# The order of two pieces of work in an FFN block: the next block's first hidden chunk and the second product's first weight block

## The chip, the cores and the metric

The kernel runs on one core of a Trainium2 chip. The metric is device time in microseconds (us) from the first to the last instruction, with what the launch adds around it; several executions are timed and the median is taken. One further execution is recorded by the hardware profiler, and its trace is what the profile shows. Engines: PE is TensorE (matmuls; PEld its weight loads), DVE is VectorE, ACT is ScalarE, POOL is GpSimd, SP issues the transfers.

## The reference, cut to what matters

One step of a two-layer decoder trunk: layer 0 mixes tokens with a gated MLP, layer 1 with a sparse attention; each is followed by the FFN below, in which the change lies. There are 1024 prompt tokens and 32 sample tokens, 1056 columns in all; the width is 1024 and the hidden width 4096.

```python
def sqrelu_mlp(h, w1, w2):
    a = jax.nn.relu(h @ w1)
    return (a * a) @ w2
...
xp = xp + sqrelu_mlp(rms_norm(xp, norm_ffn[i]), ffn_w1[i], ffn_w2[i])
xs = xs + sqrelu_mlp(rms_norm(xs, norm_ffn[i]), ffn_w1[i], ffn_w2[i])
```

## The kernel before

Every matrix is held as a high and a low part (`split`: ACT copies the high part at L203, DVE or POOL subtracts for the low part at L204), and every product takes three matmuls: high by high, high by low, low by high. Those of the projections are L242, L247 and L248, those of the second FFN product L590, L591 and L592.

`ffn` (L513 to L644) walks over 16 blocks of 256 hidden rows, `fb`. A block has two hidden tiles, `ft` 0 and 1, of 128 rows. `tile1(fb, ft)` (L607) loads a tile's weights (L211) and gives back three calls, one for each chunk of tokens (384, 384 and 288 columns; `h_69`, `h_70` and `h_71` in the rows of the order). A chunk is 24 matmuls into one PSUM buffer; `after` then makes relu times the norm's factor on DVE (L526), and the square on ACT into the staging tile `st` (L539).

The second product of a block is computed with seven instead of eight block products (Winograd's form of Strassen's scheme): tokens are cut in quarters of 264, two quarters make a pair `pr`, and seven right-hand parts of a pair stand in `A2` (`A` in the rows). Parts 0 and 1 come from tile 0 (`combine0`); parts 2 and 3 are the squares of tile 1; parts 4 to 6 are sums that POOL makes in a row of three, L556, L557, L558, each of which needs the one before. `combine1(pr)` does this, and ends with a `split` of 792 columns (ACT L203, then DVE L204). There are two pairs, so six such sums a block.

`w2_block(fb, m)` (L561) loads a block of the second weight matrix, has POOL make four sums of its quarters (L568 to L571) and splits the eight parts into `w`. `w2_pair` (L576) runs seven products for each pair, in the order of `PRODS`: v5, u1, v3, u6, q4, p2, u7. v5 and u1 need parts 1 and 0, v3 needs part 2; u6 and q4 need parts 5 and 4. u1, u6 and u7 follow one another in one PSUM buffer of the name `ps`, v5 and v3 in one of the name `px`, q4 and p2 in buffers of the name `pt`. DVE adds each finished product to `X` (L581); ACT copies u7 out (L603) and POOL adds it twice (L581).

The loop of a block that isn't the last: `combine0` for both pairs, the three chunks of tile 1 with `combine1(0)` after chunk 1 and `combine1(1)` after chunk 2, then `nxt`, the three chunks of the next block's tile 0, laid between the four calls of `w2_pair`. In the program before, chunk `m - 1` of `nxt` stands ahead of call `m`, so that the first call has none ahead of it.

What this order sets: a scheduler places the instructions of each engine by its own estimate of time, and the written order decides among those that could go. Buffers rotate: three for `raw` (transfers land there), eight for `w` (a weight tile takes two), four for `scr`, two for `st`, three each for `ps` and `px`, two for `pt`. Each engine runs its own list in order and waits on semaphores.

Of the kernel before, what the change touches and what calls it, by code (L numbers as in the profile page):

```python
# [29 lines left out]
NC = 3  # L30
# [23 lines left out]
def chunk(c):  # L54
    return slice(*CH[c])
# [75 lines left out]
def build(nc, tc, I, O):  # L131
# [12 lines left out]
    def ps(tag="ps"):  # L144
        return psp.tile([P, 512], F32, name=tag, bufs=2 if tag == "pt" else 3)

    def psd():
        rot[0] ^= 1
        return ps("px" if rot[0] else "ps")
# [40 lines left out]
    def wslot(shape, dtype=F32R):  # L190
        return wp.tile(shape, dtype, name="w", bufs=8)

    def raw(shape):
        return wp.tile(shape, F32, name="raw", bufs=3)

    def scr(w=C):
        return wp.tile([P, w], F32, name="scr", bufs=4)
# [3 lines left out]
    def split(hi, lo, src, scale=None):  # L201
        if scale is None:
            S.activation(hi, src, AF.Copy)  # L203
            (lo_w[0] or V).tensor_tensor(lo, src, f(hi), op=ALU.subtract)  # L204
        else:
            S.activation(hi, src, AF.Copy, scale=scale)
            V.scalar_tensor_tensor(lo, src, scale, f(hi), op0=ALU.mult, op1=ALU.subtract)

    def weight(src, a, b):
        r = raw([P, a, b])  # L210
        SP.dma_start(r, src)  # L211
        hi = wslot([P, a, b])
        lo = wslot([P, a, b])
        split(hi, lo, r)
        return hi, lo
# [119 lines left out]
    for k in (0, 4):  # L335
        r = raw([P, 4, 256])
        SP.dma_start(r, wA[k * P:(k + 4) * P, D:D + 256].rearrange("(z p) f -> p z f", p=P))
        for z in (0, 2):
            wt = wslot([P, 2, 2, 256])
# [98 lines left out]
    def proj_T(wsrc, o, c, wt, after, p=None):  # L438
        p = psd() if p is None else p
        p = p[:, :CH[c][1] - CH[c][0]]  # L440
        for k in range(NK):
            mm3(p, (wt[0][:, k], wt[1][:, k]), (H[c][:, k, 0], H[c][:, k, 1]), k == 0, k == NK - 1)
        after(p, o, c, chunk(c))

    def wcols(w, c0, n=P):
        return w[:, c0:c0 + n].rearrange("(k p) f -> p k f", p=P)
# [66 lines left out]
    def ffn(layer, X, fp, done):  # L513
# [9 lines left out]
        def hidden(ft, last):  # L523
            def after(p, o, c, sl):
                r = scr(sl.stop - sl.start)
                V.scalar_tensor_tensor(r, p, 0.0, rbc[:, sl], op0=ALU.max, op1=ALU.mult)  # L526
                if last and ft:
                    q = scr(sl.stop - sl.start)
                    S.activation(plain[0][:, ft, sl], r, AF.Square)
                    V.tensor_tensor(q, r, r, op=ALU.mult)  # L530
                    V.tensor_tensor(plain[1][:, ft, sl], q, f(plain[0][:, ft, sl]), op=ALU.subtract)
                    return
                a = sl.start
                while a < sl.stop:
                    pos = a // SN
                    b = min(sl.stop, (pos + 1) * SN)
                    if ft == pos % 2 == 0 and (pos // 2) not in stage:
                        stage[pos // 2] = fp.tile([P, 4, SN], F32, name="st", bufs=2)
                    S.activation(stage[pos // 2][:, SLOT[ft, pos % 2], a - pos * SN:b - pos * SN],  # L539
                                 r[:, a - sl.start:b - sl.start], AF.Square)  # L540
                    a = b
            return after
# [4 lines left out]
        def combine0(pr):  # L547
            q, t1 = stage[pr], scr(SN)[:, None]
            part(pr, 0, 1, q[:, 2:3])
            G.tensor_tensor(t1, q[:, 3:4], q[:, 2:3], op=ALU.subtract)  # L550
            part(pr, 1, 2, t1)

        def combine1(pr):
            q = stage.pop(pr)
            part(pr, 2, 4, q[:, 0:2])
            G.tensor_tensor(q[:, 3], q[:, 0], q[:, 3], op=ALU.subtract)  # L556
            G.tensor_tensor(q[:, 2], q[:, 3], q[:, 2], op=ALU.add)  # L557
            G.tensor_tensor(q[:, 1], q[:, 2], q[:, 1], op=ALU.subtract)  # L558
            part(pr, 4, 7, q[:, 1:4])

        def w2_block(fb, m):  # L561
            r = raw([P, 8, P])
            SP.dma_start(r[:, 0:4].rearrange("p (t z) o -> p t z o", t=2),
                         w2[fb * FB * P:(fb + 1) * FB * P, m * 256:(m + 1) * 256]
                         .rearrange("(t p) (z o) -> p t z o", p=P, z=2))
            a11, a21, a12, a22 = (r[:, z] for z in range(4))
            sm = [r[:, 4 + z] for z in range(4)]
            G.tensor_tensor(sm[0], a21, a22, op=ALU.add)  # L568
            G.tensor_tensor(sm[1], sm[0], a11, op=ALU.subtract)
            G.tensor_tensor(sm[2], a11, a21, op=ALU.subtract)  # L570
            G.tensor_tensor(sm[3], a12, sm[1], op=ALU.subtract)  # L571
            hi, lo = wslot([P, 8, P]), wslot([P, 8, P])
            split(hi, lo, r)
            return hi, lo

        def w2_pair(wt, m):  # L576
            bank = {}

            def add(pr, row, col, src, op=ALU.add, eng=V):
                x = X[:, 2 * m + row, (2 * pr + col) * SN:(2 * pr + col + 1) * SN]  # L580
                eng.tensor_tensor(x, x, src, op=op)  # L581

            for key, aw, bx, first in PRODS:
                for pr in range(2):
                    if first:
                        bank[key[0], pr] = ps({"u": "ps", "v": "px"}.get(key[0], "pt"))
                    p = bank[key[0], pr][:, :SN]
                    wh, wl = (w[:, aw] for w in wt)
                    xh, xl = A2h[:, pr, bx], A2l[:, pr, bx]
                    PE.matmul(p, wh, xh, start=first, stop=False, skip_group_check=not first)  # L590
                    PE.matmul(p, wh, xl, start=False, stop=False, skip_group_check=not first)  # L591
                    PE.matmul(p, wl, xh, start=False, stop=True, skip_group_check=not first)  # L592
                    if key in ("u1", "p2"):
                        add(pr, 0, 0, p)
                    elif key in ("u6", "v3"):
                        add(pr, 0, 1, p)
                    elif key == "v5":
                        add(pr, 1, 1, p)
                    elif key == "q4":
                        add(pr, 1, 0, p, ALU.subtract)  # L600
                    elif key == "u7":
                        u = scr(SN)
                        S.activation(u, p, AF.Copy)  # L603
                        add(pr, 1, 0, u, ALU.add, G)
                        add(pr, 1, 1, u, ALU.add, G)

        def tile1(fb, ft):  # L607
            wt = weight(wcols(w1, (fb * FB + ft) * P), NK, P)
            return [lambda c=c: proj_T(w1, ft, c, wt, hidden(ft, fb == nb - 1)) for c in range(NC)]

        nxt = tile1(0, 0)
        for t in nxt:
            t()
        for fb in range(nb):
            last = fb == nb - 1
            for pr in range(2):
                if last:
                    sl = slice(2 * pr * SN, 2 * (pr + 1) * SN)
                    split(plain[0][:, 0, sl], plain[1][:, 0, sl], stage.pop(pr)[:, 2:4].rearrange("p a t -> p (a t)"))
                else:  # L620
                    combine0(pr)
            for c, t in enumerate(tile1(fb, 1)):
                t()
                if c and not last:
                    combine1(c - 1)
            if not last:
                nxt = tile1(fb + 1, 0)
                for m in range(4):
                    if m:
                        nxt[m - 1]()  # L630
                    w2_pair(w2_block(fb, m), m)
                continue
            for op in range(2):
                hi, lo = weight(w2[fb * FB * P:, op * 512:(op + 1) * 512].rearrange("(t p) o -> p t o", p=P), FB, 512)
                for c in range(NC):
                    sl = chunk(c)
                    for q in range(4):
                        o = op * 4 + q
                        p = psd()[:, :sl.stop - sl.start]
                        for ft in range(FB):  # L640
                            mm3(p, (hi[:, ft, q * P:(q + 1) * P], lo[:, ft, q * P:(q + 1) * P]),
                                (plain[0][:, ft, sl], plain[1][:, ft, sl]), ft == 0, ft == FB - 1)
                        V.tensor_tensor(X[:, o, sl], p, X[:, o, sl], op=ALU.add)
                        done(o, c, sl)  # L644
# [282 lines left out]
    for h in range(NK):  # L927
        wt = weight(wcols(wB, h * P), NK, P)
# [325 lines left out]
```

## Time and profile before

| what | value |
|---|---|
| median of 3 runs | 2442.22 us (2436.52 to 2442.29) |
| profiled execution, its own time | 2439.28 us |
| its span, first to last instruction | 2436.9 us |
| PE busy | 2336.8 us, 96% |
| DVE busy | 1692.9 us, 69% |
| POOL busy | 1310.4 us, 54% |
| ACT busy | 1062.5 us, 44% |
| granted TensorE clock, mean | 0.982 |

The span lies 2.4 us under the execution's own time. A busy time is the length of the instructions' records; matmuls are pipelined, so that their records overlap, and an engine's rate is read from the distance between starts. The two FFN stages of 16 blocks lie at about 380 to 1030 us and 1740 to 2400 us of the span, the attention of layer 1 between them.

### The profile page before, as it was taken

Reading aid. Unit: us, or ns where it says so; the run is one execution under the profiler, and the core shown is the slowest. Engines: PE = TensorE matmul, PEld = TensorE weight load, DVE = VectorE, ACT = ScalarE, POOL = GpSimd, SP = SyncE. Lnnn points to the kernel's source line nnn. Section 1 sums busy time; section 2 is a strip of 40 time slices with the busy share of each in tenths; the row PEclk is TensorE's granted clock in tenths of the full one; section 3 lists DMA queues with packets and bytes.
Section 4 is the critical chain, followed back from the end, with each engine's and each line's share of the span. In section 5 each row is a group of like instructions: output and inputs, shape, how many; then the busy total and the mean of one; then the engine's idle time right before and its main releaser. Section 6 shows DMA issues by size and latency. Waiting matters only on the chain.

```text
span 2436.9 us, 42780 instructions
## 1 busy us (share of the span) xinstructions
PE 2336.8 (96%) x15961; PEld 2246.2 (92%) x15961; DVE 1692.9 (69%) x3732; ACT 1062.5 (44%) x2164; POOL 1310.4 (54%) x1695
## 2 busy tenths in 40 slices
PE   8999999999999999989988968999999999999998
PEld 7999999999999999988988747899999999999998
DVE  6151257777777777774998879735677777777775
ACT  6232243333333333355865767734333333333335
POOL 2245446676676676561224435414566766766754
PEclk9999999999999999999999979999999999999999
DMA  6211301111111111141223441040111111111111
GB/s 231 61 46 35 123 27 46 47 48 49 44 48 48 49 52 40 55 131 30 84 70 104 142 173 27 10 158 27 44 48 45 48 49 45 51 46 49 53 44 72
DMA packets 180800, 158.38 MB, mean 65 GB/s; under 512 B 10376, under 2 KB 169712, under 8 KB 179568
## 3 DMA queue, kind: packets, MB, share of 16 engines
q1 hardware_dynamic: 176496, 136.78, 18.0%
q0 software_dynamic: 4096, 18.88, 2.3%
q8 instruction: 125, 2.05, 0.4%
q14 instruction: 83, 0.68, 0.1%
HBM read 134.15 MB, written 21.47 MB: 64 GB/s over the span
## 4 chain that ended last, share of the span: by engine, by line
PE 35%; DVE 9%; POOL 4%; issue 4%; ACT 2%; DMA 1%; SPq 0%; another core or an unknown queue 0%; DVEq 0%; POOLq 0%; ACTq 0%
PE ps L242 4%; PE ps L248 4%; PE ps L247 3%; PE px L242 3%; PE px L248 3%; PE px L247 3%; PE ps L590 2%; PE ps L591 1%; PE ps L592 1%; DVE sc L895 1%; POOL st L558 1%; PE pt L1138 1%; PE pt L592 1%; PE pt L591 1%; PE pt L590 1%
## 5 line engine op out<-in xcount | busy, mean ns | idle before, releaser
L581 POOL TENSOR_TENSOR X<-X,scr 128x264 f32<-128x264 f32 x480 | 427.0, 913 | 165.0 <-DVE X L581 119.4
L248 PE MATMUL ps<-h,w 128*128 128x384 f32 (+1 forms) x1344 | 438.3, 326 | 1.6 <-POOL w L204 1.4
L242 PE MATMUL ps<-h,w 128*128 128x384 f32 (+1 forms) x1344 | 437.1, 325 | 0.7 <-DVE scr L909 0.4
L247 PE MATMUL ps<-h,w 128*128 128x384 f32 (+1 forms) x1344 | 435.8, 324 | 0.0
L203 ACT ACTIVATE w<-raw 128x1024 fp32r<-128x1024 f32 (+2 forms) x248 | 250.6, 1012 | 305.6 <-PE px L247 123.3
L204 DVE TENSOR_TENSOR w<-raw,w 128x1024 fp32r<-128x1024 f32 (+1 forms) x211 | 298.4, 1414 | 32.9 <-ACT w L203 32.6
L242 PE MATMUL px<-h,w 128*128 128x384 f32 (+1 forms) x960 | 310.8, 324 | 0.3
L248 PE MATMUL px<-h,w 128*128 128x384 f32 (+1 forms) x960 | 309.8, 323 | 0.0
L247 PE MATMUL px<-h,w 128*128 128x384 f32 (+1 forms) x960 | 309.2, 322 | 0.0
L603 ACT ACTIVATE scr<-ps 128x264 f32<-128x264 f32 x240 | 92.7, 386 | 426.4 <-PE ps L592 380.3
L248 PEld LDWEIGHTS ps<-h,w 128*128 128x128 f32 x1344 | 254.4, 189 | 3.1 <-POOL w L204 1.7
L242 PEld LDWEIGHTS ps<-h,w 128*128 128x128 f32 x1344 | 254.6, 189 | 2.4 <-ACT w L203 1.0
L247 PEld LDWEIGHTS ps<-h,w 128*128 128x128 f32 x1344 | 254.4, 189 | 0.6
L581 DVE TENSOR_TENSOR X<-X,ps 128x264 f32<-128x264 f32 x480 | 197.4, 422 | 64.3 <-PE ps L592 64.3
L581 DVE TENSOR_TENSOR X<-X,px 128x264 f32<-128x264 f32 x480 | 194.2, 422 | 52.2 <-PE px L592 52.2
L581 DVE TENSOR_TENSOR X<-X,pt 128x264 f32<-128x264 f32 x480 | 203.1, 423 | 33.7 <-PE pt L592 29.0
L590 PE MATMUL ps<-A,w 128*128 128x264 f32 x720 | 206.8, 288 | 20.2 <-ACT A L203 20.2
L591 PE MATMUL ps<-A,w 128*128 128x264 f32 x720 | 206.6, 290 | 7.6 <-DVE A L204 7.5
L592 PE MATMUL ps<-A,w 128*128 128x264 f32 x720 | 203.6, 284 | 0.0
L568 POOL TENSOR_TENSOR raw<-raw 128x128 f32<-128x128 f32 x120 | 56.6, 472 | 267.7 <-DMA raw<-in_ffn_w 178.1
L204 DVE TENSOR_TENSOR A<-st,A 128x264 fp32r<-128x264 f32 (+2 forms) x184 | 164.1, 905 | 45.7 <-ACT A L203 45.6
L242 PEld LDWEIGHTS px<-h,w 128*128 128x128 f32 x960 | 180.4, 188 | 1.3 <-DVE X L581 1.2
(397 smaller groups left out, 6326.8 us busy)
## 6 DMA issues: line engine op xcount, KB each, us to landing
raw<-in_ffn_w SPq DMA_DIRECT2D x68, 512.0 KB
raw<-in_ffn_w SPq DMA_DIRECT2D x120, 256.0 KB
X<-xd SPq DMA_DIRECT2D x16, 528.0 KB
raw<-in_a_w_in SPq DMA_DIRECT2D x10, 512.0 KB
GV<-in_x_prompt SPq DMA_DIRECT2D x8, 512.0 KB
raw<-in_a_w_out SPq DMA_DIRECT2D x8, 512.0 KB
raw<-in_b_w_in SPq DMA_DIRECT2D x8, 512.0 KB
raw<-in_b_w_out SPq DMA_DIRECT2D x8, 512.0 KB
```

The lines of the kernel that those rows point to most:

```text
L203: S.activation(hi, src, AF.Copy)
L204: (lo_w[0] or V).tensor_tensor(lo, src, f(hi), op=ALU.subtract)
L242: PE.matmul(out, lh, rh, start=first, stop=False)
L247: PE.matmul(out, lh, rl, start=False, stop=False)
L248: PE.matmul(out, ll, rh, start=False, stop=last)
L558: G.tensor_tensor(q[:, 1], q[:, 2], q[:, 1], op=ALU.subtract)
L568: G.tensor_tensor(sm[0], a21, a22, op=ALU.add)
L581: eng.tensor_tensor(x, x, src, op=op)
L590: PE.matmul(p, wh, xh, start=first, stop=False, skip_group_check=not first)
L591: PE.matmul(p, wh, xl, start=False, stop=False, skip_group_check=not first)
L592: PE.matmul(p, wl, xh, start=False, stop=True, skip_group_check=not first)
L603: S.activation(u, p, AF.Copy)
```

## The change

Ahead of the four calls of `w2_pair`, the program now loads the first second-product block (`w2_block(fb, 0)`) before it loads the next block's tile 0, and chunk `m` instead of chunk `m - 1` of `nxt` stands ahead of call `m`; there are three chunks, so the fourth call has none ahead of it. Nothing is added or taken away: each engine has the same instructions as before.

```diff
             if not last:
+                wt = w2_block(fb, 0)
                 nxt = tile1(fb + 1, 0)
                 for m in range(4):
-                    if m:
-                        nxt[m - 1]()
-                    w2_pair(w2_block(fb, m), m)
+                    if m < NC:
+                        nxt[m]()
+                    w2_pair(wt if m == 0 else w2_block(fb, m), m)
                 continue
```

On PE, where chunk 2 of tile 1 ends (`h_71`) in the fifth block of layer 0; `A_3357` is the tile of the seven parts. Before, the second product begins at once:

```order
L248 MATMUL ps<-h_71,w 128x288
L590 MATMUL px<-A_3357,w 128x264
L590 MATMUL ps<-A_3357,w 128x264
L591 MATMUL ps<-A_3357,w 128x264
L592 MATMUL ps<-A_3357,w 128x264
L590 MATMUL ps<-A_3357,w 128x264
L590 MATMUL px<-A_3357,w 128x264
L591 MATMUL ps<-A_3357,w 128x264
```

Now the next block's chunk 0 (`h_69`) follows there, two of its matmuls having gone earlier:

```order
L247 MATMUL ps<-h_71,w 128x288
L248 MATMUL ps<-h_71,w 128x288
L248 MATMUL px<-h_69,w 128x384
L242 MATMUL px<-h_69,w 128x384
L247 MATMUL px<-h_69,w 128x384
L248 MATMUL px<-h_69,w 128x384
```

So 22 matmuls of 384 columns stand between the end of tile 1 and the first product of the block, where there was none.

On PE, ahead of the first products that need parts 4 to 6, in the same block. Before, the next block's chunk 0 ends here and v3 and u6 follow (with products of the second call between):

```order
L247 MATMUL px<-h_69,w 128x384
L248 MATMUL px<-h_69,w 128x384
L590 MATMUL ps<-A_3357,w 128x264
L590 MATMUL px<-A_3357,w 128x264
L591 MATMUL px<-A_3357,w 128x264
L592 MATMUL px<-A_3357,w 128x264
L591 MATMUL ps<-A_3357,w 128x264
L592 MATMUL ps<-A_3357,w 128x264
L590 MATMUL ps<-A_3357,w 128x264
L590 MATMUL pt<-A_3357,w 128x264
```

Now 17 matmuls of chunk 1 (`h_70`) have gone ahead of v3 (the two `px` groups), and u6 (`ps`) and q4 (`pt`) come between the rest of them:

```order
L247 MATMUL ps<-h_70,w 128x384
L590 MATMUL px<-A_3357,w 128x264
L591 MATMUL px<-A_3357,w 128x264
L592 MATMUL px<-A_3357,w 128x264
L590 MATMUL px<-A_3357,w 128x264
L591 MATMUL px<-A_3357,w 128x264
L592 MATMUL px<-A_3357,w 128x264
L248 MATMUL ps<-h_70,w 128x384
L590 MATMUL ps<-A_3357,w 128x264
L590 MATMUL pt<-A_3357,w 128x264
L242 MATMUL ps<-h_70,w 128x384
```

A second chunk of the next block thus stands in the stretch that had one.

On POOL, the six sums of `combine1` in the same block. Before, pair 0's three and then pair 1's three:

```order
L550 TENSOR_TENSOR scr<-st 128x264 x2
L581 TENSOR_TENSOR X<-X,scr 128x264 x2
L556 TENSOR_TENSOR st<-st 128x264
L557 TENSOR_TENSOR st<-st 128x264
L558 TENSOR_TENSOR st<-st 128x264
L556 TENSOR_TENSOR st<-st 128x264
L557 TENSOR_TENSOR st<-st 128x264
L558 TENSOR_TENSOR st<-st 128x264
L581 TENSOR_TENSOR X<-X,scr 128x264 x4
```

Now the two pairs alternate, and a weight block's sums follow:

```order
L550 TENSOR_TENSOR scr<-st 128x264 x2
L581 TENSOR_TENSOR X<-X,scr 128x264 x2
L556 TENSOR_TENSOR st<-st 128x264 x2
L557 TENSOR_TENSOR st<-st 128x264 x2
L558 TENSOR_TENSOR st<-st 128x264 x2
L568 TENSOR_TENSOR raw<-raw 128x128
L570 TENSOR_TENSOR raw<-raw 128x128
L569 TENSOR_TENSOR raw<-raw 128x128
L571 TENSOR_TENSOR raw<-raw 128x128
```

This stands so in every other block; in the blocks between, the two pairs follow one another as before, with four sums of a weight block (L568, L570, L569 ahead of the first L556, L571 behind it) among them. In the program after, the list of DVE in the attention of layer 1 also has another order in its last third, where the last top-k selections and the first softmax steps interleave; PE, ACT and POOL have small shifts there.

## Rows read from the trace of the kernel before

**Rows 1.** The page's head: span; busy us, share of the span, instructions.
```profile
span 2436.9 us, 42780 instructions
PE 2336.8 (96%) x15961; PEld 2246.2 (92%) x15961; DVE 1692.9 (69%) x3732; ACT 1062.5 (44%) x2164; POOL 1310.4 (54%) x1695
```
**Rows 2.** Busy us by stretch: most of either FFN, and the attention between.
```profile
core 0: us, PE busy (x) PEld busy (x) DVE busy (x) ACT busy (x) POOL busy (x), PEclk, DMA share, GB/s
400.00:1010.00 610.00, 595.57 (x4203) 589.17 (x4203) 464.89 (x914) 224.25 (x461) 412.31 (x539) 1.00 0.16 48
1760.00:2360.00 600.00, 586.28 (x4136) 579.92 (x4134) 459.53 (x901) 221.25 (x456) 404.40 (x530) 1.00 0.16 48
...
1400.00:1500.00 100.00, 73.82 (x466) 51.48 (x466) 83.14 (x260) 65.49 (x168) 48.59 (x58) 0.80 0.33 116
```
**Rows 3.** Waits of PE, whole span: us in total, times, longest.
```profile
PE ps L590 <- ACT A L203: 20.2, 28, 0.8
...
PE ps L591 <- DVE A L204: 7.5, 26, 0.7
```
**Rows 4.** PE in order of time, fifth block: start, us, what, idle before.
```profile
596.07 0.28 PE L591 MATMUL px<-A,w 128*128 128x264 f32 x1
...
597.05 0.28 PE L592 MATMUL px<-A,w 128*128 128x264 f32 x1
597.58 0.39 PE L591 MATMUL ps<-A,w 128*128 128x264 f32 x1 [0.24 <-DVE A L204]
...
598.05 0.28 PE L592 MATMUL pt<-A,w 128*128 128x264 f32 x1
599.08 0.39 PE L590 MATMUL ps<-A,w 128*128 128x264 f32 x1 [0.74 <-ACT A L203]
```
**Rows 5.** The same view, where tile 1 of that block ends.
```profile
586.54 0.34 PE L242 MATMUL px<-h,w 128*128 128x384 f32 x1
586.72 0.34 PE L247 MATMUL px<-h,w 128*128 128x384 f32 x1
586.89 0.34 PE L248 MATMUL px<-h,w 128*128 128x384 f32 x1
...
590.22 0.29 PE L590 MATMUL px<-A,w 128*128 128x264 f32 x1
```
**Rows 6.** POOL in order of time, same block.
```profile
590.91 0.75 POOL L556 TENSOR_TENSOR st<-st 128x264 f32<-128x264 f32 x1 [1.26 <-ACT st L539]
591.74 1.22 POOL L557 TENSOR_TENSOR st<-st 128x264 f32<-128x264 f32 x1
593.03 0.76 POOL L558 TENSOR_TENSOR st<-st 128x264 f32<-128x264 f32 x1
593.75 1.74 POOL L556 TENSOR_TENSOR st<-st 128x264 f32<-128x264 f32 x1
595.57 1.11 POOL L557 TENSOR_TENSOR st<-st 128x264 f32<-128x264 f32 x1
596.76 1.37 POOL L558 TENSOR_TENSOR st<-st 128x264 f32<-128x264 f32 x1
```
**Rows 7.** ACT in order of time, same block.
```profile
592.45 0.52 ACT L539 ACTIVATE st<-scr 128x24 f32<-128x24 f32 x2
...
598.16 0.86 ACT L203 ACTIVATE A<-st 128x792 fp32r<-128x792 f32 x1 [3.46 <-POOL st L558]
```
**Rows 8.** DVE in order of time, same block.
```profile
593.27 1.60 DVE L204 TENSOR_TENSOR w<-raw,w 128x1024 fp32r<-128x1024 f32 x1
...
597.44 0.42 DVE L581 TENSOR_TENSOR X<-X,px 128x264 f32<-128x264 f32 x1
597.78 0.42 DVE L581 TENSOR_TENSOR X<-X,ps 128x264 f32<-128x264 f32 x1
```
**Rows 9.** Groups of the sixth block (633 to 678 us): busy us, mean ns, idle.
```profile
L581 POOL TENSOR_TENSOR X<-X,scr 128x264 f32<-128x264 f32 x18 | 16.8, 955 | 4.0 <-DVE X L581 4.0
L204 DVE TENSOR_TENSOR w<-raw,w 128x1024 fp32r<-128x1024 f32 x7 | 10.2, 1460 | 0.0
...
L568 POOL TENSOR_TENSOR raw<-raw 128x128 f32<-128x128 f32 x4 | 1.8, 460 | 9.3 <-DMA raw<-in_ffn_w 8.5 <-DVE X L581 0.8
...
L204 DVE TENSOR_TENSOR A<-st,A 128x528 fp32r<-128x528 f32 x2 | 1.6, 812 | 0.2 <-ACT A L203 0.2
```

## The prediction

> **What bounds the kernel now.** I read the page's head first [rows 1]: PE is busy for 2336.8 of 2436.9 us, so that only what keeps PE from starting its next matmul can move the time. By stretches [rows 2] both FFN stages run at a granted clock of 1.00 (2.4 GHz) with DVE busy for 76% (464.89 of 610) and POOL for 68%; the attention between them is the loose part, with PE at 73.8 of 100 us and the clock at 0.80. In the list of what PE waited for [rows 3] two waits belong to the second FFN product: L590 for ACT's part of `A`, 28 times, and L591 for DVE's part, 26 times that show. There are 30 blocks with that product.
>
> The order of time shows one of them [rows 4]. Matmuls of 264 columns start 0.1225 us apart (596.07 to 597.05 in eight steps). From 597.05 to 597.58 it is 0.53, so 0.41 us are lost, and from 598.05 to 599.08 it is 1.03, so 0.91 are lost: 1.32 us a block. The idle times that the view prints, 0.24 and 0.74, are smaller, because a record of 0.28 us reaches 0.16 beyond the next start. Twenty-eight blocks at 1.32 make **37.0 us**; from the list it is 20.2 + 7.5 + 54 x 0.16 = 36.3, so the block shown is typical. Nothing else that stands in the FFN stages is as large.
>
> Where it comes from: tile 1's last matmul is followed by the next start at 590.22 [rows 5], which I call t0. Its squares reach `st` at 592.97 [rows 7], POOL's six sums run from 590.91 to 598.13 nearly without a pause [rows 6], ACT splits pair 1's part from 598.16 on [rows 7], and PE goes on at 599.08, t0 + 8.86. PE has less than that to do meanwhile: counted in the order of before, 24 matmuls of 384 columns (0.175 us each, from 586.54 to 586.89 in two steps [rows 5]) and 27 of 264 columns stand between t0 and pair 1's first u6 matmul, 4.20 + 3.29 = 7.49 us. The missing 1.37 is the stall.
>
> **The change part by part.** The instructions are the same, so PE's own work stays and only waits can move.
>
> The moved chunk: counted in the order of after in the same way, in every other block 43 matmuls of 384 and 20 of 264 stand between t0 and that u6, 7.53 + 2.44 = 9.97 us; in the blocks between it is 37 and 24, 6.48 + 2.93 = 9.41 us. Both are over the 8.86 us after which the part was there, with 1.11 and 0.55 us to spare. In the blocks of the second kind pair 0's q4 comes early, at t0 + 5.3; pair 0's three sums were through at 593.79, t0 + 3.57, and ACT's split takes 0.86 more [rows 6, 7], t0 + 4.5. The stall goes if the chain keeps its length: **minus 37.0 us**, a bound of the gain here.
>
> The chain itself: its last sum is the sixth of six either way, so the alternation of the pairs leaves pair 1's end where it was as long as POOL works on; pair 0's last sum becomes the fifth and ends about one sum (1.37) before the sixth, at t0 + 6.5 instead of 3.6; with ACT's 0.86 that is 7.4, where PE needs it at 9.2 (40 and 18 matmuls). I take 0 here; the other end is in the rivals.
>
> The runs of products: the call that had a chunk ahead of it now has the next one's place, and the last call has none. The longest run of products without a projection matmul grows from 55 to 60 matmuls, 7.3 us of PE. In it DVE has 20 products, of which 12 in 14 are its own: 17 adds 0.34 us apart [rows 8], 5.8 us; one or two low parts of weights at 1.46 [rows 9]; and one relu of 384 columns, an estimated 0.5 by the 0.42 of an add of 264 [rows 8]: 7.8 to 9.2 us. So DVE can fall behind by 0.5 to 1.9 us, while the adds that u6 and v3 wait for leave PE only some three products, 1.1 us, ahead of it. From below the bound is 0: the run of 55 shows no wait of PE in [rows 3]. POOL in one call has four adds of 0.955 and four sums near 0.46 [rows 9], 5.7 us against PE's 14 x 3 x 0.1225 = 5.1, the same in every call as before. I take 0.2 us a block, near the lower end, because DVE is idle for 145 us in the 610 of the first stage [rows 2], 13.5 blocks by its 4203 matmuls at 312 a block, so for 10.7 us a block and 9.4 without the stall, and the run of 55 showed none: **plus 6 us** in 30 blocks; the ends are 0 and 57.
>
> The moved load: `w2_block(fb, 0)` goes onto SP's queue ahead of the next tile 0. In the order of after, its POOL sums and its low part on DVE stand in the block before, ahead of the last call's end, so both it and the tile that now comes second are there long before PE; I take 0. Without that cover it would be four sums and a low part, 4 x 0.46 + 1.46 = 3.3 us a block.
>
> Buffers: chunk 0's squares wait on ACT behind both splits of 792 columns, and its `scr` tile is held so long; there are four, and POOL's adds of u7 wait behind the six sums as they did. I take 0.
>
> The attention stretch: DVE's list has another order in its last third, with the same work. DVE is idle for 17 of 100 us there and PE for 26 [rows 2]; a worse order can lose the 17, a better one win the 26. Nothing says which, so I take 0 and keep plus or minus 8, half of DVE's idle time. The clock gives nothing in the FFN: it was granted in full there in spite of the stalls.
>
> Sum: minus 37.0 plus 6 is minus 31. The profiled execution took 2439.28, its span 2436.9; 2439.3 - 31 = **2408**. The median of the runs is 2.9 above that execution and their lowest 2.8 below it, so nothing is added.
>
> **The rivals.**
> The forecast, 2408, with its own range of 2395 (new waits of 0, and 8 from the attention) to 2420.
>
> *The chain gets longer where the pairs alternate.* In those blocks DVE's list has a low part of a weight (1.46) and two splits of 528 columns (0.81 each [rows 9]) side by side in the time of the sums. For it: L556 took 0.75 us while DVE stood and 1.74 while DVE's low part of 1.60 us ran beside it [rows 6, 8]; the six sums took 6.95 us, and three such meetings would cost up to 1.46 + 1.62 = 3.1 where the rows show about 1.6 lost already. 1.5 us more use up the 1.11 to spare. If these 14 blocks keep their stall, 14 x 1.32 = 18.5 come back: 2427. Against it: ACT makes chunk 2's squares ahead of the 528 splits now, so pair 1's sums can begin earlier.
> The Trainium skill, SBUF — State Buffer, section "Who interferes with whom", says that a VectorE instruction with two SBUF inputs and a GpSimd instruction that reads SBUF hold the shared port one at a time, and that the later one blocks fully; by it the 1.74 us would be the rest of DVE's 1.60 plus 0.75, an end at 595.62, and the trace shows 595.49, which agrees. By that rule this rival is the case in which each of the three meets a sum.
>
> *DVE becomes the bound in the runs of products, once a block.* 1.2 to 1.3 us are lost there instead: about 2439, no change. Against it: the 9.4 us that DVE has free in a block, and `px`, `ps` and `pt` hold eight products in all.
>
> *The same, at its full price (the other side).* DVE falls behind by 1.9 us in every block and nothing buffers it: 57 - 37 = plus 20, 2459. It is slower from 1.5 us a block on (37 + 7 over 30 blocks). Its place is the run of 60 between the next block's chunk 2 and tile 1's chunk 1.
>
> *The attention loses its 17 us*, with the FFN as forecast: 2425.
>
> *The change doesn't do what it says:* the scheduler could have put the chunk back. The order of after excludes it for all 30 blocks.
>
> **How the numbers follow.** A measurement of this kernel can tell about 0.3%, 7.3 us, from no change, so faster means under 2435. Forecast 0.60; the longer chain 0.15; no change by DVE 0.10; DVE at full price 0.07; the attention 0.05; the rest, 0.03, without effect. Faster: most of the forecast (0.59), most of the longer chain (0.13) and 0.04 of the attention, 0.76. The same: 0.10 + 0.03 and 0.02 of the longer chain, 0.15. Slower: 0.09. The range goes from 2395 to 2439, which leaves some 0.06 below and 0.13 above.
>
> **What would show it.** Right: the list of PE's waits has L590 for ACT and L591 for DVE at a few us instead of 27.7, a block is about 1.1 us shorter, and DVE's busy share in the FFN rises above 76%. The longer chain: the wait for `A` stays in every other block, with L556 or L557 over 1.5 us beside DVE's splits. DVE as the bound: PE waits for DVE's adds to `X` at u6 or v3 in calls 2 and 3. The attention: the stretch from 1400 on is longer or shorter by more than 5 us with the same instructions. It would be wrong altogether if PE's busy time fell short because matmuls slowed down; no row points to that.

## The result, and the profile after

The changed kernel takes **2402.49 us** (median of 4 runs, 2400.70 to 2404.09) against 2439.95 for the kernel before on the same chip (4 runs, the 3 of the table ahead of the prediction and one more): a ratio of 0.9844, 95% interval 0.9832 to 0.9857, so 1.4 to 1.7% faster. Its profiled execution took 2404.09 us, 35.2 less than that of before. The forecast was 2408, with a range from 2395 to 2439.

The page's head, which answers to [rows 1]:

```profile
span 2402.3 us, 42841 instructions
PE 2323.0 (97%) x15961; PEld 2239.6 (93%) x15961; DVE 1687.1 (70%) x3732; ACT 1056.4 (44%) x2164; POOL 1342.8 (56%) x1695
```

Each engine's count is as before (the 61 more of the first line stand in none of the five counts); the span is 34.6 us shorter. Busy times by stretch, which answer to [rows 2] (us, then busy us of PE, PEld, DVE, ACT and POOL, granted clock, DMA share, GB/s):

```profile
400.00:1010.00 610.00, 608.02 (x4326) 604.56 (x4325) 478.05 (x943) 228.07 (x476) 430.97 (x546) 1.00 0.16 49
1760.00:2360.00 600.00, 598.24 (x4256) 594.96 (x4255) 468.29 (x929) 221.67 (x461) 419.40 (x532) 1.00 0.16 48
```

In the same 610 us PE now starts 4326 matmuls instead of 4203, and it stands still for 2 us instead of 14. The gain is in the FFN. To place it, the span is cut at four marks on DVE that both kernels have: the first relu of a layer's FFN (L526), and the first add of its last block (L643 before, L644 after). The rows of these two lines, by layer, before and then after (count, ns min/median/max, first and last start):

```profile
L526 DVE SCALAR_TENSOR_TENSOR scr<-px,rbc x1: 545/545/545, 344.7 to 344.7; 128x384 f32<-128x384 f32 x1
L643 DVE TENSOR_TENSOR X<-px,X x1: 547/547/547, 1045.7 to 1045.7; 128x384 f32<-128x384 f32 x1
L526 DVE SCALAR_TENSOR_TENSOR scr<-px,rbc x1: 545/545/545, 1700.0 to 1700.0; 128x384 f32<-128x384 f32 x1
L643 DVE TENSOR_TENSOR X<-px,X x1: 558/558/558, 2398.5 to 2398.5; 128x384 f32<-128x384 f32 x1
```

```profile
L526 DVE SCALAR_TENSOR_TENSOR scr<-px,rbc x1: 542/542/542, 345.8 to 345.8; 128x384 f32<-128x384 f32 x1
L644 DVE TENSOR_TENSOR X<-px,X x1: 550/550/550, 1029.5 to 1029.5; 128x384 f32<-128x384 f32 x1
L526 DVE SCALAR_TENSOR_TENSOR scr<-px,rbc x1: 545/545/545, 1680.8 to 1680.8; 128x384 f32<-128x384 f32 x1
L644 DVE TENSOR_TENSOR X<-px,X x1: 558/558/558, 2364.8 to 2364.8; 128x384 f32<-128x384 f32 x1
```

The FFN of layer 0 goes from 701.0 to 683.7 us, that of layer 1 from 698.5 to 684.0, the stretch between them (attention above all) from 654.3 to 651.3; start and end together are unchanged to 0.2. So 31.8 of the 34.6 us came out of the FFN and 3.0 out of the middle.

In PE's waits both rows of [rows 3] are gone. The list holds idle times over 0.15 us; what is left of `A` in it is this:

```profile
PE pt L591 <- DVE A L204: 2.7, 12, 0.2
```

**A block in which the pairs alternate on POOL.** POOL and then ACT in order of time (start, us, what; x2 are two instructions in a row):

```profile
543.17 2.45 POOL L556 TENSOR_TENSOR st<-st 128x264 f32<-128x264 f32 x2 [0.53 <-ACT st L539]
545.58 2.42 POOL L557 TENSOR_TENSOR st<-st 128x264 f32<-128x264 f32 x2
547.96 1.47 POOL L558 TENSOR_TENSOR st<-st 128x264 f32<-128x264 f32 x2
548.74 1.62 ACT L203 ACTIVATE A<-st 128x792 fp32r<-128x792 f32 x2 [3.80 <-POOL st L558]
```

and PE, from the first matmul behind tile 1 (t0 = 541.68) to pair 1's first u6:

```profile
541.68 0.34 PE L248 MATMUL px<-h,w 128*128 128x384 f32 x1
...
551.61 0.28 PE L590 MATMUL ps<-A,w 128*128 128x264 f32 x1
```

The six sums take 6.26 us (543.17 to 549.43) instead of 7.22 [rows 6]. ACT's part of pair 1 is ready at 550.36, t0 + 8.68; PE comes to it at t0 + 9.93 without a pause. It is 1.25 us early where PE stood 0.91 us for it before [rows 4].

**A block of the other kind**, forty microseconds later. POOL with one of a weight block's sums (L571) between its own, then DVE, then ACT:

```profile
585.65 0.75 POOL L556 TENSOR_TENSOR st<-st 128x264 f32<-128x264 f32 x1
586.37 0.92 POOL L571 TENSOR_TENSOR raw<-raw 128x128 f32<-128x128 f32 x1
587.25 1.83 POOL L557 TENSOR_TENSOR st<-st 128x264 f32<-128x264 f32 x1
589.16 0.75 POOL L558 TENSOR_TENSOR st<-st 128x264 f32<-128x264 f32 x1
...
593.06 0.77 POOL L558 TENSOR_TENSOR st<-st 128x264 f32<-128x264 f32 x1 [1.60 <-DVE A L204]
...
587.26 1.21 DVE L204 TENSOR_TENSOR w<-raw,w 128x1024 fp32r<-128x1024 f32 x1
590.85 2.07 DVE L204 TENSOR_TENSOR A<-st,A 128x792 fp32r<-128x792 f32 x2 [2.38 <-ACT A L203]
...
589.95 1.40 ACT L203 ACTIVATE A<-st 128x792 fp32r<-128x792 f32 x2 [2.04 <-POOL st L558]
...
594.00 0.85 ACT L203 ACTIVATE A<-st 128x792 fp32r<-128x792 f32 x1
```

and PE there (t0 = 585.30):

```profile
590.48 0.28 PE L592 MATMUL ps<-A,w 128*128 128x264 f32 x1
590.87 0.39 PE L590 MATMUL pt<-A,w 128*128 128x264 f32 x1
...
591.79 0.33 PE L247 MATMUL ps<-h,w 128*128 128x384 f32 x1
592.35 0.39 PE L591 MATMUL pt<-A,w 128*128 128x264 f32 x1 [0.23 <-DVE A L204]
```

Pair 0's q4 should have started at 590.60 and starts at 590.87; its second matmul, which needs DVE's part, is 0.39 us late again. The matmul behind each pause starts 0.1 us further off than usual too, so it is 0.27 + 0.10 + 0.39 + 0.11 = 0.87 us, in every other block (12 in all). It is nearly all that PE still loses in the FFN.

Pair 1's part is late in these blocks too. Its last sum (593.06) waits 1.60 us for DVE, whose second split from 590.85 on still reads the square that this sum overwrites. ACT's part is ready at 594.85, t0 + 9.55. PE comes to pair 1's u6 at 595.55, t0 + 10.25, without a pause, but only because q4's pauses have held it back by 0.87.

What PE loses can be counted over all blocks: the distance from each matmul's start to the next, less 0.175 us for 384 columns, 0.133 for 288 and 0.122 for 264. Between the marks PE loses 22.1 + 21.6 = 43.7 us in the two FFN stages before, and 5.1 + 5.5 = 10.6 after. The difference, 33.1, is the stage gain of 31.8 and another 1.2: between the marks lie 7 matmuls of 384 columns more after the change than before (3058 against 3051). This "loss of PE" is given for the experiments too; time at the lower clock counts in it, which matters in one of them.

### The profile page after: what moved, and what is told of

Same layout as the page of the kernel before. It is cut to its first block, busy times and chain, and to the rows that moved or that the text cites. A ratio compares the mean times of both kernels' runs of the same rounds, so it can differ in the third digit from the quotient of the medians.

```text
span 2402.3 us, 42841 instructions
## 1 busy us (share of the span) xinstructions
PE 2323.0 (97%) x15961; PEld 2239.6 (93%) x15961; DVE 1687.1 (70%) x3732; ACT 1056.4 (44%) x2164; POOL 1342.8 (56%) x1695
## 4 chain that ended last, share of the span: by engine, by line
PE 38%; DVE 7%; POOL 4%; issue 2%; DMA 2%; ACT 2%; SPq 0%; POOLq 0%; DVEq 0%; ACTq 0%
PE ps L242 4%; PE ps L248 4%; PE ps L247 4%; PE px L242 3%; PE px L247 3%; PE px L248 3%; PE ps L591 2%; PE ps L590 2%; PE ps L592 2%; POOL X L581 1%; DVE sc L896 1%; PE pt L591 1%; PE pt L1139 1%; PE px L592 1%; PE px L591 1%
## 5 line engine op out<-in xcount | busy, mean ns | idle before, releaser
L581 POOL TENSOR_TENSOR X<-X,scr 128x264 f32<-128x264 f32 x480 | 461.9, 987 | 323.5 <-ACT scr L603 293.9
L204 DVE TENSOR_TENSOR w<-raw,w 128x1024 fp32r<-128x1024 f32 (+1 forms) x211 | 282.2, 1338 | 52.6 <-ACT w L203 52.2
L581 DVE TENSOR_TENSOR X<-X,px 128x264 f32<-128x264 f32 x480 | 188.4, 421 | 55.6 <-PE px L592 55.2
L591 PE MATMUL ps<-A,w 128*128 128x264 f32 x720 | 205.3, 285 | 0.0
L590 PE MATMUL ps<-A,w 128*128 128x264 f32 x720 | 205.2, 285 | 0.0
L247 PEld LDWEIGHTS px<-h,w 128*128 128x128 f32 x960 | 180.8, 188 | 0.1
L242 PEld LDWEIGHTS px<-h,w 128*128 128x128 f32 x960 | 180.7, 188 | 0.1
```

The costliest lines, as they stand in the source:

```text
L242: PE.matmul(out, lh, rh, start=first, stop=False)
L247: PE.matmul(out, lh, rl, start=False, stop=False)
```

## The experiments

The runs e1 to e4 were made on one chip, e5 to e8 on a second and e9 to e12 on a third, each time beside the kernel before, whose medians there were 2438.94, 2440.31 and 2439.32; each ratio is to the kernel before on the same chip. Stage lengths are read at the four marks above, in each kernel's profiled execution, to more digits than the rows above print.

| kernel | median us | ratio (95% interval) | FFN 0 | between | FFN 1 | loss of PE in the two FFN |
|---|---|---|---|---|---|---|
| before | 2439.95 | 1 | 700.9 | 654.4 | 698.5 | 43.7 |
| changed (after) | 2402.49 | 0.9844 (0.9832 to 0.9857) | 683.7 | 651.4 | 684.0 | 10.6 |
| the same, e1 | 2403.11 | 0.9848 (0.9834 to 0.9861) | 683.6 | 650.3 | 684.0 | 10.5 |
| the same, e12 | 2400.93 | 0.9845 (0.9831 to 0.9858) | 683.6 | 650.2 | 683.9 | 10.4 |
| load alone, e2 | 2445.75 | 1.0023 (1.0012 to 1.0033) | 703.5 | 652.1 | 701.3 | 49.1 |
| chunks alone, e3 | 2398.12 | 0.9829 (0.9816 to 0.9842) | 680.8 | 651.6 | 681.1 | 4.9 |
| chunks alone, e10 | 2399.71 | 0.9843 (0.9829 to 0.9856) | 680.7 | 653.6 | 681.1 | 4.8 |
| two chunks ahead, e4 | 2412.72 | 0.9886 (0.9871 to 0.9901) | 687.3 | 653.3 | 687.9 | 18.2 |
| the same, no load ahead, e11 | 2412.44 | 0.9888 (0.9872 to 0.9903) | 687.6 | 652.6 | 687.9 | 17.4 |
| changed, p2 early, e5 | 2399.79 | 0.9832 (0.9819 to 0.9845) | 681.0 | 652.7 | 681.3 | 4.5 |
| chunks alone, p2 early, e9 | 2403.07 | 0.9852 (0.9838 to 0.9865) | 682.9 | 653.4 | 683.3 | 9.0 |
| before, p2 early, e6 | 2426.62 | 0.9946 (0.9933 to 0.9959) | 695.7 | 649.1 | 695.0 | 36.3 |
| before, one more sum, e7 | 2483.82 | 1.0183 (1.0162 to 1.0205) | 731.8 | 652.5 | 715.9 | 92.0 |
| changed, one more sum, e8 | 2416.45 | 0.9903 (0.9889 to 0.9917) | 690.4 | 649.1 | 690.2 | 23.5 |

### The measure: the changed kernel again

> The changed kernel, unaltered, as the measure for the runs beside it. Every theory: 2400 to 2406 us, with the wait for A of about 0.27 to 0.4 us at pair 0's q4 in every other block and none at u6.

> The changed kernel once more on this chip, as the measure for the three beside it: 2400 to 2405 us.

Measured 2403.11 and 2400.93. The FFN stages repeat to 0.1 us, the stretch between them to about 1.

### The parts of the change apart

The load alone:

```diff
                 for m in range(4):
-                    if m < NC:
-                        nxt[m]()
+                    if m:
+                        nxt[m - 1]()
                     w2_pair(wt if m == 0 else w2_block(fb, m), m)
```

> Only the first weight block of the second product is loaded ahead of the next tile 0; the chunks stand as before the change. Cover theory (the time went because 22 matmuls of a chunk now stand between the end of tile 1 and the first u6 of pair 1): pair 1's u6 comes 6.4 to 7.5 us after the end of tile 1, as before the change, its part is ready at 8.9, so the wait of about 1.3 us a block stays: 2433 to 2447 us, the list of PE's waits with some 20 us at L590 for ACT's A. Rival, the load (the wait was in truth for weights that came late): the gain is here, 2400 to 2412. Rival, the scheduler (any edit would have put the list into a better order): somewhere between, with the attention stretch shorter by 3 us or more.

Measured 2445.75: not only no gain but 0.23% more than before, and both FFN stages are 2.6 and 2.8 us longer. The waits for `A` are all there:

```profile
PE ps L590 <- ACT A L203: 21.1, 29, 0.8
PE ps L591 <- DVE A L204: 6.9, 23, 0.7
```

Where the load's extra time arises is seen in one block, on POOL and DVE behind the chain of sums:

```profile
598.16 0.46 POOL L568 TENSOR_TENSOR raw<-raw 128x128 f32<-128x128 f32 x1
...
599.53 1.08 POOL L571 TENSOR_TENSOR raw<-raw 128x128 f32<-128x128 f32 x1
...
599.13 1.16 DVE L204 TENSOR_TENSOR A<-st,A 128x792 fp32r<-128x792 f32 x1 [0.86 <-ACT A L203]
```

The weight block now lands earlier, so that its four sums start where POOL stood idle before; they run beside DVE's split of pair 1, which takes 1.16 us. In the same block of the kernel before it was this:

```profile
599.05 0.98 DVE L204 TENSOR_TENSOR A<-st,A 128x792 fp32r<-128x792 f32 x1 [0.86 <-ACT A L203]
```

The second matmul of pair 1's u6 needs that split. It and the one behind it are 0.12 + 0.10 us late, where it was 0.04: 0.18 us, and 5.4 us in 28 blocks are 0.19 each. The block shown is typical: the split of pair 1 takes 0.98 us in all 30 blocks before, and 1.15 or 1.16 in 26 of the 30 with the load ahead.

The chunks alone:

```diff
             if not last:
-                wt = w2_block(fb, 0)
                 nxt = tile1(fb + 1, 0)
                 for m in range(4):
                     if m < NC:
                         nxt[m]()
-                    w2_pair(wt if m == 0 else w2_block(fb, m), m)
+                    w2_pair(w2_block(fb, m), m)
```

> Only the chunks move: chunk m of the next tile 0 ahead of call m, the load of the first weight block behind the next tile 0 as before the change. Cover theory: pair 1's u6 comes 8.0 to 8.7 us after the end of tile 1 in two blocks of three and 9.3 to 9.8 in the rest; with the part ready at 8.7 to 8.9 between 0 and 0.9 us stay, 0.4 on the mean, so 28 x 0.9 = 25 of the 37 us go: 2408 to 2418 us, with waits at u6 or q4 in some of the blocks. Rival, the load: no gain, 2433 to 2447. If the load's place costs nothing at all: 2400 to 2406 as with both.

> The moves of the chunks alone once more, as the measure for its neighbours: 2396 to 2401 us, below the changed kernel's 2400 to 2405 on the same chip if the load's place is what costs.

Measured 2398.12 beside e1's 2403.11, and 2399.71 beside e12's 2400.93. So the whole gain comes from the chunks. The expectation of e3 was too pessimistic on the cover: the first matmul of a u6 or q4 no longer pauses for `A`, and the second of a u6, which needs DVE's part, is 0.03 to 0.20 us late in 7 blocks. What every third block still loses, 0.27 us, is another wait: a product needs a `ps` buffer that ACT's copy of u7 has to free first. PE there, and then the copy:

```profile
520.07 0.28 PE L592 MATMUL ps<-A,w 128*128 128x264 f32 x1
520.46 0.39 PE L590 MATMUL ps<-A,w 128*128 128x264 f32 x1
...
520.02 0.39 ACT L603 ACTIVATE scr<-ps 128x264 f32<-128x264 f32 x1 [2.13 <-PE ps L592]
```

Between the marks the load ahead costs 683.6 + 684.0 - 680.8 - 681.1 = 5.7 us in the changed kernel, as it cost 5.4 in e2. Of these, 5.0 show in the medians of one chip and 1.2 in those of the other; the stretch between the FFN stages takes 1.3 and 3.4 us back. That is under 0.3% either way, so which kernel is faster isn't settled by the medians; that the load ahead lengthens the FFN stages is, by four profiles that repeat to 0.1 us.

### More cover than needed

Two chunks ahead of the first call, with the load ahead, and the same without it (e11 leaves `wt` out):

```diff
                 nxt = tile1(fb + 1, 0)
+                nxt[0]()
                 for m in range(4):
-                    if m < NC:
-                        nxt[m]()
+                    if m + 1 < NC:
+                        nxt[m + 1]()
```

> Chunks 0 and 1 of the next tile 0 stand ahead of the first call, chunk 2 ahead of the second, nothing ahead of the last two; the load is ahead as in the change. Cover theory: pair 1's u6 comes 13.4 us after the end of tile 1 and pair 0's q4 9.5, so neither waits, and the 0.66 us that every other block still loses at q4 goes (12 x 0.66 = 8 us): 2392 to 2398 us. Rival, the product run: the run of products without a projection between them grows from 60 to some 80 matmuls, DVE falls behind and PE waits for DVE's adds to X; at the price that the prediction held for possible (up to 1.9 us a block) it is 2400 to 2450, and PE's waits on DVE X or on px and ps buffers show it.

> Two chunks ahead of the first call as in the earlier kernel, but with the load behind the next tile 0. If the long run of products (96 matmuls) is what lost there, with DVE's adds late, PE still waits some 0.4 us a block for DVE's X: 2408 to 2414 us. If the load's place lost it: 2396 to 2402.

Measured 2412.72 and 2412.44: the rival's case, and not by the load. The wait for `A` is nearly gone and another has its place, in e4 once a block:

```profile
PE ps L590 <- DVE X L581: 6.5, 28, 0.3
```

DVE and PE at one of these (DVE's rows first):

```profile
515.40 1.22 DVE L204 TENSOR_TENSOR w<-raw,w 128x1024 fp32r<-128x1024 f32 x1
...
518.25 1.51 DVE L204 TENSOR_TENSOR w<-raw,w 128x1024 fp32r<-128x1024 f32 x1
519.68 0.42 DVE L581 TENSOR_TENSOR X<-X,ps 128x264 f32<-128x264 f32 x1
...
519.63 0.28 PE L592 MATMUL pt<-A,w 128*128 128x264 f32 x1
520.16 0.39 PE L590 MATMUL ps<-A,w 128*128 128x264 f32 x1 [0.24 <-DVE X L581]
```

In e4 PE makes 96 product matmuls in a row; DVE's adds stand behind two low parts of weights, and the third `ps` buffer isn't free until the add at 519.68 has read it. It is the mechanism that the prediction priced for runs of 60. At 60 (the changed kernel) and in the runs of 66 and 78 of e3 no wait on DVE's `X` in the product shows in PE's list (by the starts, e3 has one of 0.24 us in each layer); at 96 it is 0.41 + 0.10 us a block. In e11 the runs are of 93 and 94, and it is some 0.64 + 0.11 us in every other block; in the blocks between, q4 waits for ACT's part again, mostly for 0.1 to 0.2 us.

### Another cover: p2 early

```diff
-PRODS = (("v5", 4, 1, True), ("u1", 0, 0, True), ("v3", 7, 2, False), ("u6", 5, 5, False), ("q4", 3, 4, True),
-         ("p2", 2, 3, True), ("u7", 6, 6, False))
+PRODS = (("v5", 4, 1, True), ("u1", 0, 0, True), ("v3", 7, 2, False), ("p2", 2, 3, True), ("u6", 5, 5, False),
+         ("q4", 3, 4, True), ("u7", 6, 6, False))
```

> The changed kernel with one difference in the list of the seven products: p2, which needs only part 3 and none of POOL's sums, stands ahead of u6 and q4. Cover theory: q4 comes at 10.4 us or later after the end of tile 1 and u6 at 9.2 to 10.0, so the wait of 0.66 us at pair 0's q4 in every other block goes: 2392 to 2398 us. Rival (the rest is not that wait but the way in which the products share px, ps and pt): 2400 to 2406, with waits on other buffers.

Measured 2399.79, a ratio of 0.9832 against the changed kernel's 0.9844 to 0.9848. The loss of PE falls from 10.6 to 4.5 us and the pause at q4 is gone; the FFN is 5.4 us shorter than in the changed kernel, but the middle stretch is longer by 1 to 2.5. So the time misses its expectation by 2 us, above. The cover theory forecast that the pause would go, but this run doesn't test it alone: with p2 early POOL's list has another order too, and from the fifth block of each layer on the pairs alternate in every block, as at 632 us, where the changed kernel has every other block of the other kind:

```profile
632.32 2.46 POOL L556 TENSOR_TENSOR st<-st 128x264 f32<-128x264 f32 x2 [0.52 <-ACT st L539]
```

The blocks in which q4 came too early no longer occur, so how much p2 would have covered in them isn't shown.

> The kernel before the change with p2 ahead of u6 and q4, chunks and load as before. Cover theory: two products of three matmuls come ahead of the late parts, so pair 0's are in time and pair 1's u6 or q4 comes 0.7 to 1.1 us later than before: 28 blocks of that are 20 to 30 us of the 37: 2410 to 2420 us, and the wait at L590 for A is smaller but there. Rival, the chunk is needed for something else than cover (the weights, the squares): 2436 to 2443, no gain.

Measured 2426.62: a gain, in the place that was named, but 13.7 us instead of 20 to 30, and only 8.7 of them in the FFN. The reason is in the waits:

```profile
PE ps L591 <- DVE A L204: 14.5, 28, 0.6
```

The wait moved from L590 to L591. A u6 product needs ACT's part of `A` for its first matmul and DVE's part for the second, and DVE splits only after ACT: in the kernel before at 599.05, for 0.98 us, where ACT ended at 599.02 [rows 7]. My expectation reckoned with the first part only; the second is a further microsecond late. In the changed kernel it did not matter: in the block with t0 = 541.68 the first matmul of pair 1's u6 starts at 551.61 and the second at 552.68, with eight others between. A smaller part of the missing gain stands at `pt` products, which start 0.04 to 0.29 us late (once 0.56) behind DVE's adds to `X` in most blocks of e6, though its runs of products are of 60 as well.

> The moves of the chunks alone (the load stays behind the next tile 0), with p2 ahead of u6 and q4. The FFN stages of the chunks alone still lose 2.3 and 2.6 us, nearly all at the first u6 in every third block, which p2 delays by another 0.37 us for each pair. If that is all that is left: 2394 to 2398 us. If the order of the lists costs as much as it gives: 2397 to 2402.

Measured 2403.07, above both. The loss of PE rises from 4.8 to 9.0 us. About half of it now stands at `px` products (2.0 us in either layer), where PE's list names DVE's adds to `X` as the releaser:

```profile
PE px L590 <- DVE X L581: 1.1, 2, 0.6
```

The expectation took what e3 still loses for a wait at the first u6; the rows of e3 show it at a `ps` buffer. The rest was not followed up. The two covers don't add.

### The chain made longer

One more POOL sum, of a tile of zeros, in pair 1's chain (`none` is 128x264, set once):

```diff
             G.tensor_tensor(q[:, 3], q[:, 0], q[:, 3], op=ALU.subtract)
+            if pr == 1:
+                G.tensor_tensor(q[:, 3], q[:, 3], none, op=ALU.add)
             G.tensor_tensor(q[:, 2], q[:, 3], q[:, 2], op=ALU.add)
```

> The kernel before the change with one more POOL sum of 264 columns in pair 1's chain (adding a tile of zeros), in all 30 blocks with the second product. If POOL's chain of sums sets when PE goes on, each block is later by the sum's whole time, 0.75 us alone to 1.74 beside DVE: 30 blocks make plus 22 to plus 50 us, 2462 to 2490. If the wait had another cause (the weights, ACT's splits), the sum costs under 7 us: 2440 to 2447.

> The changed kernel with the same additional POOL sum. Cover theory: pair 1's part was ready 1.3 us ahead of its u6 in the blocks where the pairs alternate and some 0.7 in the others, so a sum of 0.75 us or more is hidden in the first and at most half shown in the second: plus 0 to plus 10 us, 2400 to 2413. If the chain still sets the time: plus 22 to plus 50, 2424 to 2453.

On the kernel before it costs 43.5 us (2483.82 against 2440.31), inside the range that was expected, but only half of it for the reason that was given. The chain does set when PE goes on: the pause at u6 is 1.73 us instead of 0.91, so 0.82 more, 23 us in 28 blocks. On the changed kernel it costs some 14 us, the ratio 0.9903 against 0.9846. That is above the 0 to 10 that I expected; the FFN stages are 12.9 us longer than in the changed kernel, 0.43 us a block. In the blocks with the slack of 1.25 us it costs 0.2 (two starts 0.1 further off); in the others the pauses at `pt` and `ps` grow from 0.87 to some 1.3:

```profile
PE pt L594 <- ACT A L205: 5.3, 14, 0.4
```

The rest of the 43.5 on the kernel before is the clock, which no expectation held. Busy times by stretch of e7 (the last three columns are the granted clock, DMA share and GB/s):

```profile
400.00:1010.00 610.00, 585.55 (x4002) 578.58 (x4001) 446.72 (x869) 211.67 (x435) 394.28 (x524) 0.97 0.15 45
1760.00:2360.00 600.00, 578.81 (x4043) 573.65 (x4042) 447.87 (x881) 213.93 (x441) 405.57 (x532) 0.99 0.15 47
...
516.00:517.00 1.00, 1.00 (x6) 1.00 (x7) 1.00 (x2) 0.00 (x0) 0.00 (x0) 0.71 0.00 0
517.00:518.00 1.00, 1.00 (x7) 1.00 (x7) 1.00 (x4) 0.00 (x0) 0.00 (x0) 0.50 0.00 0
518.00:519.00 1.00, 1.00 (x6) 1.00 (x6) 0.99 (x3) 0.00 (x0) 0.00 (x0) 0.50 0.00 0
519.00:520.00 1.00, 1.00 (x7) 1.00 (x6) 0.53 (x2) 0.01 (x1) 0.00 (x0) 0.58 0.00 0
...
560.00:565.00 5.00, 3.44 (x27) 3.22 (x27) 3.32 (x8) 0.86 (x1) 2.02 (x2) 1.00 0.32 95
```

At 515.97 PE comes out of a pause of 1.72 us and runs on at 1.2 GHz (0.50) until about 519.8: 0.29 + 0.50 + 0.50 + 0.42 = 1.7 us lost. After the next pause of the same length, at 563.04, the clock stays full. Three per cent of 610 and one per cent of 600 are 24 us. In the profiled execution the two FFN stages are 48.3 us longer than before: 23 in the pauses, and 24 for the clock is about what is missing. Before the change, with pauses of 0.91, the clock was 1.00 over both stretches [rows 2]; so the stall of before did not cost clock, and the longer one did after some of its pauses.

## Why the prediction was right, and where its steps were off

**The stall: right.** Minus 37.0 was the largest term, and the two waits have left PE's list. The arithmetic behind it held: where the pairs alternate, pair 1's u6 was put at t0 + 9.97 and comes at t0 + 9.93, its part was put at t0 + 8.86 and is ready at 8.68. The size was a little short: the matmul behind each pause starts late as well, 0.11 + 0.10 + 0.04 us in the block of [rows 4], so that PE's whole loss of before was 43.7, of which the chunks alone take away 38.8 (e3). That it is cover, and not the weights or a lucky order, is shown from three sides: the chunks alone bring all of it and the load alone none (e3, e2); a sum put into the chain makes the pause 0.82 us longer in every block before, and 0.2 to 0.5 after, where there is slack (e7, e8); and another cover, p2, takes part of it away at the same place on the kernel before (e6).

**The longer chain where the pairs alternate: fell there, and came in the other blocks.** Where they alternate the six sums take 6.26 us instead of 7.22. The meetings with DVE are there (two L556 in 2.45 us, two L557 in 2.42, where one alone takes 0.75), but the last two meet nothing (1.47 for two), and no time passes between the sums. In the other blocks, which this rival left out, the chain did not keep its length: pair 1's part is ready at t0 + 9.55, against the 8.86 of the sum and the need at 9.41. The 0.55 us to spare were used up there, and the pause at q4 hides it.

**Pair 0's early q4: mis-sized.** The sum held t0 + 4.5 for its part against a need at t0 + 5.3. The need was right (590.60 is t0 + 5.30); the part came at t0 + 5.5, since L571 (0.92) stands among pair 0's sums and L557 took 1.83 where the row used had 1.22 [rows 6]. L557 ran beside a low part on DVE, from 587.26 for 1.21 us. By the rule of the Trainium skill, SBUF — State Buffer, section "Who interferes with whom", on a two-input VectorE instruction and a GpSimd instruction that reads SBUF, the later of the two waits; if that was L557, it would end 0.75 us behind DVE's 588.47, at 589.22. The trace shows 589.08, close to it. Which came first the starts don't tell, 0.01 us apart and POOL's ahead; that POOL waited is read from DVE's 1.21 us, no longer than the 1.22 that this instruction takes beside an idle POOL. With DVE's half of the split behind it the block loses 0.87 us, every other block.

**The moved load: the step that failed.** I took 0, since weights and tile would still be there in time; so they are. What the load also moves is POOL's sums of that block, into the stretch in which POOL and DVE make `A`. Its price is 5.4 us (e2) to 5.7 (e3 against the changed kernel). In the changed kernel it shows as the pause at q4, which is gone without the load ahead (e3). The order shown ahead of the prediction had L571 between the sums; I read it and gave it no time.

**The run of products: too dear.** I took plus 6, with 57 as the upper end. At the 60 matmuls of the changed kernel no pause for DVE's adds is seen in PE's list; at 96 it is 0.5 us a block (e4). The mechanism was real and named rightly, in buffers and in DVE's low parts, and 1.9 us a block was never near. These two errors, 0 for 5.6 and 6 for 0, cancel, and that is why the sum stood so close; this was luck.

**The attention: 0 plus or minus 8, measured minus 3.0.** Over all kernels the stretch between the FFN stages lies between 649.1 and 654.4 us though its instructions are the same, and for one and the same kernel it moved by 1.2 us (after, e1, e12) and by 2.0 (e3, e10). So minus 3.0, against a single profile of the kernel before, is hardly more than the repeats differ by, and whether the new order of DVE's list gained anything isn't shown; half the margin would have done.

**Rivals.** That DVE cancels the gain needed 1.2 us a block; even 96 matmuls in a row gave 0.5. "Doesn't do what it says" fell with the profile.

The sum read minus 31; measured were minus 35.2 in the profiled executions and minus 37.5 by the medians. Of the 35.2, PE's loss in the FFN accounts for 33.1: minus 38.8 by the chunks and plus 5.7 by the load. The rest lies outside the FFN stages.

## What to carry to other kernels

Where one engine waits for a chain on others, count what stands between the chain's start and the first instruction that needs its end, in that engine's own time, and compare it with the chain's length: here 7.49 us of cover before and 9.93 after, against a chain of 8.7 to 8.9 us, told the outcome to some tenths. Do it for every kind of block: a change that helps one can lengthen the chain in the next. Check the need for each operand apart, since the second part of a split comes later than the first. And follow a moved load to the work that it starts on other engines: weights that were in time anyway came earlier, their sums fell among those that mattered, and the load was the one part of the change that cost.

## What the runs showed of the hardware

A pause of 1.72 us on TensorE, once in some 46 us, brought the granted clock down to 1.2 GHz for about 3.4 us after some of the pauses and not after others (0.97 and 0.99 as the means of the two FFN stretches in e7), while pauses of 0.91 us at about the same distance left it at 1.00. The 0.82 us that a sum added to each block became 1.45 us of time in the mean. So a stall can be worth more than its length.
